# Two of the sample's turns beside the first projections instead of three, and the second chunk's first weights fetched with its rows

## The chip, the cores and the metric

One core of a Trainium2 chip runs the kernel. It has a matrix engine (TensorE, PE in the profile, with PEld for its weight loads), VectorE (DVE), ScalarE (ACT), GpSimd (POOL) and a queue that issues most transfers (SyncE, SP). The metric is the device time of one launch in microseconds (us), the median of several runs.

## What is computed

One inference step of a four-part hybrid decoder, for a prompt of 2048 tokens and a sample of 8 sequences with 8 new tokens each, whose 4096 past keys and values lie in a paged cache. Width 1024, 16 heads of 64. A recurrent layer comes first, then keys, values and forget gates are projected once, then one attention layer reads them. Cut to what matters here:

```python
def run_group(x, ...):
    y = recurrent_mixer(rms_norm(x, a_pre_norm), ..., a_w_in, ..., a_w_out)   # causal conv, RG-LRU, gate
    x = x + rms_norm(y, a_post_norm)
    k, v, logf = shared_kv(x, kv_norm, w_kv, b_f)
    # the sample's keys: cache_k[page_table] with the new rows behind them; the same for v and logf
    z = rms_norm(x, b_pre_norm) @ b_w_in
    q, g = z[..., :D_ATTN], z[..., D_ATTN:]
    s = q @ k.T * HEAD_DIM ** -0.5 + cq - ck          # cumulated log forget gates, causal mask
    o = softmax(s) @ v
    return x + rms_norm((o * silu(g)) @ b_w_out, b_post_norm), k, v, logf, ...
```

## The kernel before

Products with weights are made of three matmuls each, on high and low halves of both operands (lines 383 to 385), so each weight is fetched (`fetch`, line 415, tile `wst`) and then split in two (`wh` on ACT, `wl` on DVE or POOL). `Feed` (line 444) holds a list of weights in the order of their use: its `fetch` starts loads as far as the staging pool named in `wpool` has free buffers, and its `take` splits what is not yet split.

The prompt goes through the recurrent layer in two chunks of 1024 tokens (the first with the sample's 64 rows). The program's stages, in order:

- the recurrent layer of the first chunk (`recur`, `phase_a1`, then `phase_a2`);
- the first projections (`shared`, `phase_b`): keys, queries, values and gates of the first chunk. The generator yields after each group of 24 matmuls, 120 steps in all. The groups are called `kv` (rows as output) and `qg` (features as output); gates leave through tile `tgb` to `sgd` (line 974);
- the recurrent layer of the second chunk, the projections of two further chunks of 512, attention over 64 units, and the last projection.

The sample's attention against its cache is cut into 16 turns (a sequence and half of the heads each, `decode`, line 1043). A turn loads 32 pages of keys and 32 of values of 256 KB each (tile `raw`, line 1093), turns the keys on DVE (`ktr`, line 1180), makes scores (`dS`, line 1148), a softmax and products (`dO`, line 1262), and ends with a small product `dres` (line 1290). `FIRST` of the turns stand beside the first projections, from step 41 on: `Side.along` (line 1029) takes steps of the turns in proportion to the cost of the projections' steps, at a share that grows with `FIRST`, so that the turns' cost is used up about ten steps before `LEFT` = 16 steps remain. The other turns stand beside the later projections and attention, again in proportion to cost (`SHARE`, `SPAN`), and end before attention does.

When the first turns are recorded, their pool is closed (line 1817), and on its memory come the second chunk's staging pool for weights (`stage2`, line 1818) and its rows (`Norm0`, line 1819, tile `xt`, loaded at line 544, scaled at line 568, transposed on PE at line 524 into `tps`). `AHEAD` = 8 steps of the projections are then recorded, the first rows are transposed, and the rest of the projections follows. `recur` makes the feed for the recurrent layer's input weights and fetches from it as its first action, after all that.

The order within each engine's queue is not the order of the code: the framework records the instructions and a scheduler sorts them by a timeline that it simulates. On the chip each engine and each queue takes its instructions strictly in that order.

Of the kernel before, what the change touches and what calls it, by code (L numbers as in the profile page):

```python
# [22 lines left out]
KB = 8  # L23
# [28 lines left out]
SHARE0 = 2.0  # L52
LEFT = 16
AHEAD = 8
FIRST = 3
NACC = 5
NP = 6
ADD = "G"
# [29 lines left out]
def tile_hawk_fox(  # L88
# [72 lines left out]
    def super_chunks(sizes, width):  # L161
        assert sum(sizes) == SEQ
        return [SC(i, sum(sizes[:i]), n, width) for i, n in enumerate(sizes)]

    sca, scb = super_chunks(CHUNKS_A, 384), super_chunks(CHUNKS_B, 512)
# [56 lines left out]
    def sbuf(es, name, side=None):  # L222
        return es.enter_context(tc.tile_pool(name=name, bufs=1, side=side, reuse_waits="tile"))
# [165 lines left out]
    wpool = {"st": sbuf(stage, "stage", "right"), "ns": 3}  # L389
# [12 lines left out]
    class Weights:  # L402
# [28 lines left out]
        def ready(self):  # L431
            while len(self.t) < 2:
                if len(self.st) == len(self.t):
                    self.fetch()
                self.split()
            return self
# [66 lines left out]
    def alloc_x(pool, cols, g=""):  # L503
        return tuple(pool.tile([P, KB, cols], F32R, name=f"x{x}", tag=f"x{x}{g}") for x in "hl")

    def alloc_groups(pool, s, lo, hi):
        return [alloc_x(pool, s.groups[g][1], g) for g in range(lo, hi)]
# [1233 lines left out]
    a_in = [[(0, a_w_in[0, :, n * P:(n + 1) * P]), (P, a_w_in[0, :, D + n * P:D + (n + 1) * P])] for n in range(KB)]  # L1741
# [4 lines left out]
        todo[0][0].append((256, w_kv[:, 2 * D:]))  # L1746
        return todo

    def recur(s, a0, xs, covered, ex, out, then, begin, ready=None):

        with ExitStack() as ek:
            wk = sbuf(ek, f"a1_{s.i}")
            xs.extend(alloc_groups(sbuf(ex, f"xa_{s.i}"), s, len(xs), len(s.groups)))
            feed = Feed([(a_in[n],) for n in range(KB)])
            feed.fetch()
            feed.fetch()
            if ready:
                ready()

            def turnover():  # L1760
                ex.close()
                then()

            phase_a1(s, xs, a0, covered, feed, wk, out, turnover, begin)
# [11 lines left out]
    def steps(gen, n):  # L1776
        for _ in range(n):
            next(gen)
# [3 lines left out]
    a00 = Norm0(sca[0], sbuf(es0, "a0_0", "right"))  # L1782
    todo = a00.norm(2)
    out = Out(a_w_out[0], 4)
    x0, a2 = [], []
# [4 lines left out]
        out.place(sbuf(wo, "wo_0", "right"))  # L1790

    xs = []
    recur(sca[0], a00.turned(xs, todo), xs, 0, ExitStack(), out, turn0, lambda: next(a2[0]), prologue)
    x0.extend(alloc_x(sbuf(xe0, "xb0"), scb[0].cols))
    drain(a2[0])
    wo.close()
    turns = [(b, 0) for b in range(FIRST)]
    turns += [(b, hg) for b in range(DB) for hg in range(2) if (b, hg) not in turns]
# [14 lines left out]
    dec = ExitStack()  # L1813
    side = Side(decode(dec, turns[:FIRST], 2, 2, False))
    side.along(gen, FIRST * TURN / 320000 * SHARE0, 120 - done - LEFT)
    side.upto(1e12)
    dec.close()
    wst = sbuf(stage, "stage2", "right")
    a01 = Norm0(sca[1], sbuf(es1, "a0_1", "right"))
    todo = a01.norm(3)  # L1820
    ex, xs = ExitStack(), []
    xs.extend(alloc_groups(sbuf(ex, "xg_1", "right"), sca[1], 0, 1))
    steps(gen, AHEAD)
    a01 = a01.turned(xs, todo)
    covered = next(a01)
# [6 lines left out]
    out = Out(a_w_out[0], 4)  # L1832
    x1, a2 = [], []
    lim, end = scb[1].g0, scb[1].g0 + scb[1].cols

    def turn1():
# [2 lines left out]
                           lambda g: (*(t[:, (g - lim) // P] for t in x1), 0) if g < end else (g - end,)))  # L1839
        out.place(sbuf(wo, "wo_1", "right"))  # L1840

    recur(sca[1], a01, xs, covered, ex, out, turn1, lambda: next(a2[0]))
    xpool = sbuf(xe1, "xb1")
    x1.extend(xpool.tile([P, scb[1].cols // P, KB, P], F32R, name=f"x{x}", tag=f"x{x}") for x in "hl")
    drain(a2[0])
# [16 lines left out]
    def beside():  # L1862
        yield from decode(dec, turns[FIRST:], 4, 2, True)
        dec.close()
        dec_done.append(True)
        yield from project_ready(last)

    side = Side(beside())
    share = SHARE * (16 - FIRST) * TURN / (1024 / 128 * 24 * 4112 * 0.42 + 950000)
    side.along(gen, share)  # L1870
# [4 lines left out]
    cost = sum(4.1 * 0.42 * (512 - max(0, k - qc * 4) * P) + 213 for qc in range(4) for k in range(4 * qc + 4)) * H  # L1875
    side.along(attention(att), ((16 - FIRST) * TURN - side.spent) / (cost * SPAN))
    place.clear()
# [14 lines left out]
def build(inputs):  # L1892
    import numpy as _np
    import concourse.bacc as _bacc
    import concourse.tile as _tile
    from concourse import mybir as _mybir

    nc = _bacc.Bacc("TRN2", target_bir_lowering=False, num_devices=1)
    arrays, args = {}, []
    for name in _INS:  # L1900
        a = _np.ascontiguousarray(inputs[name])
        arrays[f"in_{name}_dram"] = a
        args.append(nc.dram_tensor(f"in_{name}_dram", a.shape, _mybir.dt.from_np(a.dtype), kind="ExternalInput").ap())
    for i, shape in enumerate(_OUTS):
        args.append(nc.dram_tensor(f"out_{i}_dram", shape, F32, kind="ExternalOutput").ap())
    with _tile.TileContext(nc, schedule_with_timeline_sim=True) as tc:
        tile_hawk_fox(tc, *args)
    return nc, arrays
# [8 lines left out]
```

## Time and profile before

| | us |
|---|---|
| median of 3 runs | 3024.01 |
| lowest and highest run | 3018.45, 3026.65 |
| span of the profiled execution (first to last instruction) | 3014.0 |
| the profiled execution's own time (launch to end) | not recorded beside its span |
| mean granted clock of TensorE | 0.970 of full speed |

A table by group of instructions gives their busy time, the mean of one, and the idle time of the engine just ahead of them with what ended it. The timeline gives start, duration, engine, line, operation, and the tiles (written <- read), with the count of equal neighbours. A table of stretches gives for each stretch the busy time of every engine, the granted clock, the share of time in which the 16 transfer engines were busy, and what they moved. A profile lists each matmul on 32-bit data of dS, dO and their like as two entries, so the program's order has half as many.

### The profile page before, as it was taken

The numbers are of one execution on the slowest core, as the hardware profiler recorded it, in microseconds if no ns is written. First come the engines' busy times: TensorE is split into PE (matmuls) and PEld (weight loads), VectorE is DVE, ScalarE is ACT, GpSimd is POOL, SyncE is SP. The second block draws the span as 40 slices with busy tenths as digits, with TensorE's granted clock in tenths as the row PEclk, the third lists the DMA queues.
The fourth block names the chain that finished last, engine by engine and source line by source line (L and its number), as shares of the span: only waits on it lengthen the run. The fifth ranks groups of instructions, "written<-read, shape, count | busy, mean of one in ns | idle before, by whom it ended". The sixth has DMA issues, their size and how long they took to land.

```text
span 3014.0 us, 60435 instructions
## 1 busy us (share of the span) xinstructions
PE 2787.3 (92%) x21614; PEld 2240.2 (74%) x21614; DVE 1802.1 (60%) x4013; ACT 1268.1 (42%) x2874; POOL 1084.5 (36%) x1198
## 2 busy tenths in 40 slices
PE   5998999999987999999999689999899999999998
PEld 5997789989877997888889456666566556566687
DVE  7877465424427775676564466767566656655344
ACT  4665342222125665534333234444444444355311
POOL 1653201000003653100000246666575756569522
PEclk9999999999998999999999889999999999999999
DMA  4224546889863226699999868888699877874343
GB/s 123 83 85 134 175 124 195 251 275 282 269 218 92 90 90 194 210 318 344 340 334 322 271 225 243 258 282 285 212 290 292 268 251 252 275 249 122 95 148 111
DMA packets 472958, 653.78 MB, mean 217 GB/s; under 512 B 91291, under 2 KB 268828, under 8 KB 465381
## 3 DMA queue, kind: packets, MB, share of 16 engines
q1 hardware_dynamic: 470950, 644.26, 67.2%
q10 hardware_dynamic: 1420, 3.56, 0.4%
q8 instruction: 171, 2.80, 0.4%
q0 software_dynamic: 288, 2.10, 0.2%
q14 instruction: 129, 1.06, 0.1%
HBM read 514.22 MB, written 135.16 MB: 215 GB/s over the span
## 4 chain that ended last, share of the span: by engine, by line
PE 59%; DMA 17%; DVE 9%; ACT 5%; SPq 4%; issue 3%; POOL 2%; DVEq 0%; ACTq 0%; POOLq 0%
PE ops L1622 6%; DMA raw<-in_cache_k_dram 5%; PE y L383 4%; PE st L1594 4%; PE y L384 4%; PE y L385 4%; PE sx L1429 4%; PE dO L1262 3%; PE kv L383 3%; PE kv L384 3%; PE kv L385 3%; PE st L1595 3%; PE dS L1148 3%; DMA raw<-in_cache_v_dram 3%; PE qg L383 2%
## 5 line engine op out<-in xcount | busy, mean ns | idle before, releaser
L108 POOL TENSOR_TENSOR acc<-acc,p 128x512 f32<-128x512 f32 (+3 forms) x543 | 599.3, 1105 | 331.4 <-PE ops L1622 143.4
L1609 ACT ACTIVATE p<-st 128x512 f32<-128x512 f32 (+2 forms) x553 | 278.0, 526 | 394.4 <-PE st L1595 187.4
L1180 DVE STREAM_TRANSPOSE ktr<-raw 128x1024 f32<-128x1024 f32 x256 | 307.8, 1225 | 126.1 <-DMA raw<-in_cache_k_dram 115.6
L1431 DVE TENSOR_REDUCE mxs<-sx 128x1 f32<-128x512 f32 x384 | 254.0, 681 | 144.4 <-PE sx L1429 143.5
L384 PE MATMUL kv<-wl,xh 128*128 128x256 f32 (+3 forms) x1088 | 307.6, 285 | 5.6 <-DVE wl L428 5.6
L383 PE MATMUL kv<-wh,xh 128*128 128x256 f32 (+3 forms) x1088 | 308.1, 287 | 4.5 <-ACT wh L427 4.5
L385 PE MATMUL kv<-wh,xl 128*128 128x256 f32 (+3 forms) x1088 | 307.4, 284 | 2.5 <-DMA xl<-xld 2.5
L1594 PE MATMUL st<-qa,ka 128*128 128x512 f32 (+3 forms) x640 | 269.7, 423 | 11.3 <-ACT p L1609 8.7
L1429 PE MATMUL sx<-kbt,qbt 96*128 96x512 f32 (+3 forms) x640 | 225.6, 413 | 48.5 <-DMA qbt<-qd 30.8
L1622 PE MATMUL ops<-p,vvt 128*64 128x256 f32 (+1 forms) x2090 | 253.3, 369 | 0.7 <-ACT p L1609 0.4
L1113 POOL TENSOR_TENSOR qw<-qb,amask 128x128 f32<-128x128 f32 x64 | 31.2, 493 | 606.5 <-PE dS L1148 313.0
L427 ACT ACTIVATE wh<-wst,gv 128x256 fp32r<-128x256 f32 (+1 forms) x384 | 164.5, 499 | 197.3 <-DMA wst<-in_b_w_in_dram 59.7
L428 DVE SCALAR_TENSOR_TENSOR wl<-wst,gv,wh 128x256 fp32r<-128x256 f32 (+1 forms) x384 | 169.0, 494 | 129.5 <-ACT wh L427 113.3
L1595 PE MATMUL st<-qbt,kbt 128*128 128x512 f32 (+3 forms) x640 | 236.6, 371 | 0.1
L383 PE MATMUL qg<-xh,wh 128*128 128x512 f32 (+2 forms) x640 | 229.0, 359 | 0.0
L385 PE MATMUL qg<-xh,wl 128*128 128x384 f32 (+2 forms) x640 | 227.9, 357 | 1.1 <-DVE wl L428 1.1
L384 PE MATMUL qg<-xl,wh 128*128 128x512 f32 (+2 forms) x640 | 227.7, 357 | 0.0
L1622 PEld LDWEIGHTS ops<-p,vvt 128*64 128x64 f32 x2090 | 155.2, 141 | 84.2 <-issue 20.0
L383 PEld LDWEIGHTS kv<-wh,xh 128*128 128x128 f32 (+1 forms) x1088 | 201.5, 187 | 11.6 <-ACT wh L427 6.2
L384 PEld LDWEIGHTS kv<-wl,xh 128*128 128x128 f32 (+1 forms) x1088 | 202.0, 187 | 9.7 <-DVE wl L428 6.5
L385 PEld LDWEIGHTS kv<-wh,xl 128*128 128x128 f32 (+1 forms) x1088 | 203.2, 187 | 4.3 <-DMA xl<-xld 2.9
L1594 PEld LDWEIGHTS st<-qa,ka 128*128 128x128 f32 x640 | 124.2, 194 | 104.1 <-issue 51.1
(307 smaller groups left out, 6399.2 us busy)
## 6 DMA issues: line engine op xcount, KB each, us to landing
raw<-in_cache_k_dram SPq DMA_DIRECT2D x512, 256.0 KB
raw<-in_cache_v_dram SPq DMA_DIRECT2D x512, 256.0 KB
wst<-in_w_kv_dram SPq DMA_DIRECT2D x48, 512.0 KB
wst<-in_b_w_in_dram SPq DMA_DIRECT2D x48, 512.0 KB
xt<-in_x_prompt_dram SPq DMA_DIRECT2D x32, 512.0 KB
wst<-in_a_w_in_dram SPq DMA_DIRECT2D x64, 256.0 KB
out_dram<-kf SPq DMA_DIRECT2D x128, 128.0 KB
sc<-cd SPq DMA_DIRECT2D x16, 1024.0 KB
```

The source lines that it names most:

```text
L108: eng.tensor_tensor(out, a, b, op=op)
L383: T.matmul(ps, lh(k), rh(k), start=(k == 0), stop=False)
L384: T.matmul(ps, lh(k), rl(k), start=False, stop=False)
L385: T.matmul(ps, ll(k), rh(k), start=False, stop=(k == nk - 1))
L428: V.scalar_tensor_tensor(wl[:, k, :], st[:, k, :], gk, f(wh[:, k, :]), op0=ALU.mult, op1=ALU.subtract)
L1180: behind("V", V.transpose(t.kts[pp][:, n], raw[:, :, pp * 256:(pp + 1) * 256]).ins)
L1429: T.matmul(ps[:, :w], qb[0:96, j * P:(j + 1) * P], kb[0:96, ck * 512:ck * 512 + w], start=True, stop=True)
L1431: place["V"] = V.reduce_max(mx[:, j, ck:ck + 1], ps[:, :w], axis=AX.X).ins
L1594: place["T"] = T.matmul(ps[:, lo:], ka[:, ks], qa[:, lo:], start=True, stop=False).ins
L1595: T.matmul(ps[:, lo:], kb[:, ks], qb[:, lo:], start=False, stop=(k < qc * 4))
L1609: pair.append((k, lo, p, A.activation(p[:, lo:], ps[:, lo:], AF.Exp)))
L1622: return T.matmul(ops[r * HD:(r + 1) * HD, a0 * P:], vvs[h % 2][:, k, :], p[:, :].rearrange("p (a r c) -> p a r c", a=2, r=2)[:, a0:, r, : ...
```

## The change

`FIRST` becomes 2: the third turn leaves the first projections and joins the others, which become 14. The shares of both sides are formulas in `FIRST` and change with it. The feed of the second chunk's recurrent layer is made and asked to fetch directly behind the allocation of its rows, into `stage2`, and handed to `recur`; the staging pool of the projections still to be recorded is put back after that.

```diff
-FIRST = 3
+FIRST = 2
...
-    def recur(s, a0, xs, covered, ex, out, then, begin, ready=None):
+    def input_weights():
+        feed = Feed([(a_in[n],) for n in range(KB)])
+        feed.fetch()
+        feed.fetch()
+        return feed
+
+    def recur(s, a0, xs, covered, feed, ex, out, then, begin, ready=None):
...
-            feed = Feed([(a_in[n],) for n in range(KB)])
-            feed.fetch()
-            feed.fetch()
+            feed = feed or input_weights()
...
-    recur(sca[0], a00.turned(xs, todo), xs, 0, ExitStack(), out, turn0, lambda: next(a2[0]), prologue)
+    recur(sca[0], a00.turned(xs, todo), xs, 0, None, ExitStack(), out, turn0, lambda: next(a2[0]), prologue)
...
     xs.extend(alloc_groups(sbuf(ex, "xg_1", "right"), sca[1], 0, 1))
+    of_b, wpool["st"], wpool["ns"] = dict(wpool), wst, 3
+    feed = input_weights()
+    wpool.update(of_b)
     steps(gen, AHEAD)
...
-    recur(sca[1], a01, xs, covered, ex, out, turn1, lambda: next(a2[0]))
+    recur(sca[1], a01, xs, covered, feed, ex, out, turn1, lambda: next(a2[0]))
```

Three places in the order of the built programs. First, SP's queue around the second chunk's rows (`xt`), before: behind the last pages of the third turn come the last three stores of gates, then rows and weights.

```order
L1093 DMA raw<-in_cache_v_dram 128x512
L974 DMA sgd<-tgb 128x256
L974 DMA sgd<-tgb 128x384
L683 DMA gst<-in_a_w_ga_dram 128x128
L684 DMA gst<-in_a_w_gx_dram 128x128
L974 DMA sgd<-tgb 128x384
L544 DMA xt<-in_x_prompt_dram 128x1024
L536 DMA apreB<-in_a_pre_norm_dram 128x1024
L544 DMA xt<-in_x_prompt_dram 128x1024 x3
L415 DMA wst<-in_a_w_in_dram 128x4x128 x6
```

The same queue in the changed program, from the second store behind the last pages of the second turn on:

```order
L974 DMA sgd<-tgb 128x384
L415 DMA wst<-in_b_w_in_dram 128x4x256
L544 DMA xt<-in_x_prompt_dram 128x1024
L536 DMA apreB<-in_a_pre_norm_dram 128x1024
L544 DMA xt<-in_x_prompt_dram 128x1024
L974 DMA sgd<-tgb 128x256
L544 DMA xt<-in_x_prompt_dram 128x1024 x2
L415 DMA wst<-in_a_w_in_dram 128x4x128 x6
L974 DMA sgd<-tgb 128x384 x2
L974 DMA sgd<-tgb 128x256
L974 DMA sgd<-tgb 128x384
L415 DMA wst<-in_b_w_in_dram 128x4x256
```

Rows and input weights now stand ahead of 17 of the stage's stores and of the last weight of the gates.

Second, PE's queue at the end of the first projections, before (`u` and `g` are the recurrent layer's first products):

```order
L383 MATMUL qg<-xh,wh 128x384
L384 MATMUL qg<-xl,wh 128x384
L385 MATMUL qg<-xh,wl 128x384
L1290 MATMUL dres<-sel,ob 128x16 x4
L524 MATMUL tps<-ident,xt 128x128 x24
L383 MATMUL u<-xh,wh 128x384
L383 MATMUL g<-xh,wh 128x384
```

In the changed program the last turn's `dres` has 219 `qg` matmuls between it and the first eight transposes; the last eight of the first 24 stand like this among the projections:

```order
L384 MATMUL qg<-xl,wh 128x384
L385 MATMUL qg<-xh,wl 128x384
L383 MATMUL qg<-xh,wh 128x320
L384 MATMUL qg<-xl,wh 128x320
L524 MATMUL tps<-ident,xt 128x128 x4
L385 MATMUL qg<-xh,wl 128x320
L524 MATMUL tps<-ident,xt 128x128 x4
L383 MATMUL qg<-xh,wh 128x320
```

From there to the last `qg` are 141 more, and `u` follows it directly; in all 411 `qg` stand between `dres` and `u`, where there were none.

Third, PE's queue at the start of attention (`sx`, the first pass over the scores), before and then changed:

```order
L384 MATMUL qg<-xl,wh 128x512
L385 MATMUL qg<-xh,wl 128x512
L1226 MATMUL dsum<-ddg,ones 128x64
L1429 MATMUL sx<-kbt_19861,qbt_19862 128x128
L1429 MATMUL sx<-kbt_19861,qbt_19862 128x256
```

The changed queue has the scores of a turn where the sum of a softmax stood:

```order
L385 MATMUL qg<-xh,wl 128x512
L1148 MATMUL dS<-ktr,qw 32x128 x32
L1163 MATMUL dS<-sy,qw 32x8 x16
L1148 MATMUL dS<-ktr,qw 32x128 x32
L1429 MATMUL sx<-kbt_19536,qbt_19537 128x128
```

Counted over these rows, 656 instead of 576 dS and 198 instead of 188 dO stand between the recurrent layer and attention's first `sx`, and 1360 instead of 1296 and 726 instead of 670 behind it.

## The prediction

> **What bounds the kernel now.** I read the page's first part, then a table of stretches cut at the stages, then the timeline at the seam between the first chunk's projections and the second chunk's recurrent layer, because both edits act there. First the page:
>
> ```profile
> PE 2787.3 (92%) x21614; PEld 2240.2 (74%) x21614; DVE 1802.1 (60%) x4013; ACT 1268.1 (42%) x2874; POOL 1084.5 (36%) x1198
> ```
>
> TensorE (PE) is the busiest engine by far, so time is won or lost where PE works less or stands still. The table of stretches has, after the length, the busy time of PE, PEld, DVE, ACT and POOL with instruction counts, then granted clock, DMA share and GB/s:
>
> ```profile
> 520.00:893.00 373.00, 351.52 (x3491) 330.26 (x3489) 147.99 (x265) 89.89 (x244) 7.09 (x23) 1.00 0.83 258
> 893.00:926.00 33.00, 9.14 (x40) 7.69 (x40) 18.15 (x45) 15.64 (x34) 10.94 (x7) 0.59 0.83 250
> ...
> 1290.00:1707.00 417.00, 407.28 (x3744) 351.91 (x3742) 258.43 (x507) 156.45 (x404) 21.71 (x35) 1.00 0.99 327
> 1707.00:1748.00 41.00, 8.86 (x23) 4.93 (x27) 8.81 (x29) 2.44 (x9) 8.28 (x13) 0.54 0.91 241
> 1748.00:2720.00 972.00, 918.23 (x8323) 585.39 (x8317) 634.07 (x1342) 442.96 (x1094) 599.48 (x569) 0.97 0.82 260
> 2720.00:2840.00 120.00, 117.19 (x661) 77.94 (x658) 56.29 (x115) 61.44 (x133) 92.37 (x81) 0.96 0.31 94
> ```
>
> From 520 to 893 the first chunk's projections run with three of the sample's turns beside them; from 1290 to 1707 the later projections, and from 1748 attention, run with the other thirteen. PE is busy 94 to 98% in all three, so a turn costs its PE time wherever it stands. Two holes remain: 893 to 926 and 1707 to 1748. The first is the seam. PE's timeline there (start, us, operation, count, and in brackets the idle time before it and what ended it):
>
> ```profile
> 892.67 0.96 PE L1290 MATMUL dres<-sel,ob 128*128 128x16 f32 x8
> 910.03 1.97 PE L524 MATMUL tps<-ident,xt 128*128 128x128 f32 x8 [16.40 <-DVE xt L568]
> 917.05 1.97 PE L524 MATMUL tps<-ident,xt 128*128 128x128 f32 x8 [5.05 <-DVE xl L108]
> 921.42 2.21 PE L524 MATMUL tps<-ident,xt 128*128 128x128 f32 x8 [2.41 <-DVE xl L108]
> ...
> 932.71 1.03 PE L524 MATMUL tps<-ident,xt 128*128 128x128 f32 x8
> 934.85 1.32 PE L524 MATMUL tps<-ident,xt 128*128 128x128 f32 x8 [1.10 <-DVE xl L108]
> 939.17 1.97 PE L524 MATMUL tps<-ident,xt 128*128 128x128 f32 x8 [3.00 <-DVE xl L108]
> ```
>
> PE ends the third turn (dres) at 893.6 and then waits for the second chunk's rows, normalised on DVE. Why so late is in the timeline of the other queues:
>
> ```profile
> 879.58 2.02 SPq L1093 DMA_DIRECT2D raw<-in_cache_v_dram  x4
> 882.60 5.87 SPq L974 DMA_DIRECT2D sgd<-tgb  x2
> ...
> 894.40 0.42 SPq L544 DMA_DIRECT2D xt<-in_x_prompt_dram  x1
> ...
> 897.08 7.69 SPq L415 DMA_DIRECT2D wst<-in_a_w_in_dram  x6
> ```
> ```profile
> 908.69 5.91 DVE L568 SCALAR_TENSOR_TENSOR xt<-xt,nr_y,apreB 128x1024 f32<-128x1024 f32 x3
> ```
> ```profile
> 908.79 3.40 POOL L108 TENSOR_TENSOR wl<-wst,wh 128x1024 fp32r<-128x1024 f32 x1 [12.08 <-ACT wh L101]
> ```
>
> The third turn's last pages are asked for at 880, its last product is at the very end of the projections, and rows and input weights, which take over the turns' buffers, are asked for only after that: 894.4 and 897.1. Loading, squaring and scaling three rows' tiles takes to 914.6, twenty microseconds with nothing left for PE.
>
> **The change, part by part.** *(a) One turn leaves the first stage.* PE's work for a turn is the key scores (dS) and the value products (dO). The table of stretches for each alone (length, PE, PEld, DVE or ACT busy, clock, DMA), dS first, then dO:
>
> ```profile
> 520.00:893.00 373.00, 25.56 (x864) 23.85 (x864) 8.79 (x15) 1.00 0.83 258
> 1290.00:1712.00 422.00, 35.98 (x1152) 31.35 (x1152) 11.74 (x20) 0.99 0.99 327
> 1748.00:2720.00 972.00, 83.73 (x2592) 73.17 (x2592) 26.71 (x45) 0.97 0.82 260
> ```
> ```profile
> 520.00:893.00 373.00, 26.33 (x396) 12.05 (x396) 1.09 (x3) 1.00 0.83 258
> 1290.00:1712.00 422.00, 25.57 (x376) 10.54 (x376) 0.73 (x2) 0.99 0.99 327
> 1748.00:2720.00 972.00, 94.42 (x1340) 37.78 (x1332) 4.08 (x11) 0.97 0.82 260
> ```
>
> A turn is 288 dS and 132 dO entries. In the first stage it costs (25.56 + 26.33)/3 = 17.3 us. The waits of PE ahead of these groups, and ahead of the projections' own matmuls, in 520 to 893:
>
> ```profile
> L383 PE MATMUL kv<-wh,xh 128*128 128x256 f32 (+1 forms) x504 | 142.3, 285 | 2.3 <-ACT wh L427 2.3
> L384 PE MATMUL kv<-wl,xh 128*128 128x256 f32 (+1 forms) x504 | 142.3, 284 | 2.9 <-DVE wl L428 2.9
> ...
> L1262 PE MATMUL dO<-raw,sx 128*32 128x256 f32 x384 | 25.1, 384 | 7.7 <-DMA raw<-in_cache_v_dram 4.2 <-issue 1.3 <-DMA vd<-kf 1.2
> L1148 PE MATMUL dS<-ktr,qw 128*32 128x128 f32 x768 | 22.4, 273 | 3.8 <-DVE ktr L1180 3.8
> ```
>
> So (7.7 + 3.8)/3 = 3.8 of waiting goes too: **-21.1**. The projections' own waits, 2.3 + 2.9 = 5.2, come of sharing ACT, DVE and the DMA with the turns; between 0 and -5.2, and I take a third, **-1.7**.
>
> *(b) It comes back later.* The order rows put 80 more dS and 10 more dO ahead of attention, 64 and 56 inside it; each is two trace entries. Before attention: 160 x 35.98/1152 + 20 x 25.57/376 = 6.4. Inside: 128 x 83.73/2592 + 112 x 94.42/1340 = 12.0. The waits in attention:
>
> ```profile
> L1262 PE MATMUL dO<-raw,sx 128*32 128x256 f32 x1296 | 88.6, 394 | 13.2 <-DMA raw<-in_cache_v_dram 13.2
> L1148 PE MATMUL dS<-ktr,qw 128*32 128x128 f32 x2304 | 73.1, 281 | 3.3 <-DVE oTs L108 3.3
> ```
>
> At that rate 112/1296 x 13.2 + 128/2304 x 3.3 = 1.3 more. Together **+19.7**. The turn's small products (dm, dsum, dres) and its exponentials go and come alike. Its 64 page loads of 256 KB stay on the same queue, only later; whether the DMA has room is not in this sum. Lower bound 0, since these stages hardly wait for pages; upper bound, if pages bind, in the rivals. I take **+2**, near the waits seen.
>
> *(c) The seam.* With two turns the second ends, in the order, 411 projection matmuls before the stage's end. Their pace:
>
> ```profile
> 860.00:893.00 33.00, 26.43 (x148) 24.27 (x148) 3.19 (x6) 2.93 (x7) 1.00 0.69 224
> ```
>
> 26.43/148 = 0.18 us each, so some 74 us of PE work lie behind the turn and 219 x 0.18 = 39 us between it and the first transpose of rows. Loading and scaling took 20 us at the seam; it fits beneath. The window 893 to 926 holds 9.14 of PE work at clock 0.59, worth 5.4 at full clock, so 27.6 of its 33.0 go. Of the next rows' waits (1.10 and 3.00) I take half, 2, since two transpose buffers still pace them. Against this stands a wait of 0 to 4.5: the first weights have their data early, but their second half needs a buffer that the stage's last weights hold until their last use, and then POOL's 3.40 (the row above) and ACT's rounding of about 1; the first half's 24 matmuls cover most. I take 2. Together **-27.6**, from -32 to -23.
>
> The Trainium skill, "TensorE: Matmul & The Clock Gate", "HAM oscillation", says only an idle stretch of more than about 3.4 us halves the clock, so by the page a residual wait of 2 costs 2 and no more. The rows at 932.71 and 939.17 show eight transposes at 1.03 without a wait and 1.97 after 3.00, so by the trace it could cost 0.9 on top, and the sum would be -26.7.
>
> The six weight loads of the second edit pass about eighteen stores of gates and the last weights on SP's queue. If SP stands at a load because a turn's buffer is not free, stores behind it wait, then the gate buffers, then PE: the cover is the four PSUM buffers of a group each, 24 x 0.18 = 4.3 us a group, some 17 us; past that each microsecond is PE's. By the order the turn is over by then, so I cost it at 0.
>
> *(d) The other hole*, 1707 to 1748, waits for attention's first keys behind page traffic. Another phase of a turn will stand there (scores instead of exponentials and their scattered stores). I have no row for that phase: -10 to +10, value 0.
>
> **Sum** against the profiled execution: -21.1 - 1.7 + 19.7 + 2 - 27.6 = -28.7, span 3014.0 to 2985.3. The median of the runs, 3024.0, lies 10.0 above the span (start and end around it, which no row shows); I keep that: **2995 us**.
>
> **Rivals.** *The seam stays.* The second turn lags on the chip as the third did (its V pages landing late), or rows and weights still come after the last store. Then only -1.1 remains: 3023. For it: now, too, the end of the turns is a matter of pages. Against: 411 matmuls of distance instead of none. A half closed seam gives 3009.
>
> *Attention becomes bound by the turns' pace: slower.* PE takes its queue in order, so if a turn cannot run faster than now, attention stretches to hold more of them. Two turn ends there:
>
> ```profile
> 2567.72 1.02 PE L1290 MATMUL dres<-sel,ob 128*128 128x16 f32 x8
> ...
> 2664.38 0.96 PE L1290 MATMUL dres<-sel,ob 128*128 128x16 f32 x8
> ```
>
> 96.7 us a turn. Inside attention 0.44 of a turn's scores and 0.85 of its products are added, 0.65 on the mean: 63 us instead of 13.3, so +21 in all: 3045. It decides from about 29 us of added waiting. Against it: PE waits 16.5 us for dS and dO in 972, so the turns have slack now; for it, the DMA share is 0.82 there and 0.99 in the stage ahead. The DMA view of 1290 to 1707 in 40 slices:
>
> ```profile
> GB/s 301 370 294 284 360 327 326 267 303 332 403 358 389 379 376 279 333 368 398 259 358 320 261 359 338 369 352 331 328 305 284 373 322 318 309 363 355 355 208 174
> ```
>
> Slices of 403 and 398 against a mean of 327 show room. The Trainium skill, "DMA: Bandwidth & Descriptors", "Specifications", gives about 358 GB/s from HBM for one core; taken as a limit it would leave this stage 31 GB/s and make the rival likelier; the slices above it, stores included, say it isn't one here.
>
> **How the numbers follow.** Forecast 0.72, 2995, own range 2978 to 3007 by its bounds; half closed seam 0.09, 3009; seam stays 0.12, 3023; attention slower 0.07, 3045. About 0.3% is what a measurement of this kernel tells from no change, 9 us: faster means below 3015, which the first two give, 0.81; same 0.12; slower 0.07. The range runs from 2978 to 3022, leaving out the last case, part of the third and the forecast's low tail.
>
> **What would show it.** Right: no idle above 3 us on PE where tps first stands, transposes between qg matmuls, clock near 1.00 through the seam, wst<-in_a_w_in issued some 60 us before the last gate store; dS x576 and dO x264 in the first projections; waits before dO in attention near 15. Wrong: a tps wait of over 10 us, dS or dO waits in attention that double, or a hole before attention that grows beyond 50.

## The result, and the profile after

| | before | changed |
|---|---|---|
| median of 6 runs each, us | 3021.23 | 2999.76 |
| lowest to highest | 3014.74 to 3031.76 | 2996.61 to 3001.49 |
| span of the profiled execution | 3014.0 | 2998.0 |

The ratio is 0.994, with a 95% interval of 0.9919 to 0.996: 0.4 to 0.8% faster, 18 us by the ratio and 21 by the medians. The forecast was 2995.

The page's first part for the changed kernel: PE does the same work as before.

```profile
PE 2789.2 (93%) x21614; PEld 2245.0 (75%) x21614; DVE 1800.9 (60%) x4013; ACT 1265.0 (42%) x2874; POOL 1078.6 (36%) x1198
```

The table of stretches, with the columns as before (length, PE, PEld, DVE, ACT, POOL, clock, DMA share, GB/s):

```profile
800.00:875.00 75.00, 75.00 (x467) 74.63 (x464) 37.55 (x95) 30.79 (x72) 4.33 (x8) 1.00 0.49 157
875.00:910.00 35.00, 31.03 (x177) 29.42 (x176) 19.28 (x39) 13.18 (x26) 8.82 (x13) 0.90 0.21 62
1208.00:1673.00 465.00, 449.45 (x3988) 387.62 (x3987) 289.88 (x608) 175.85 (x448) 22.73 (x49) 0.99 0.98 324
1673.00:1710.00 37.00, 9.65 (x173) 6.98 (x171) 12.50 (x32) 1.08 (x2) 8.80 (x14) 0.64 0.92 289
1710.00:2690.00 980.00, 915.31 (x8475) 584.46 (x8474) 642.14 (x1362) 436.83 (x1094) 587.37 (x564) 0.97 0.85 270
```

The seam lies at 875 now. PE is busy without a break in the 75 us ahead of it, and 31 of the 35 us behind it; where 33 us held 9 us of work at clock 0.59 before, the clock is now 0.90. The queue of transfers shows why:

```profile
804.11 0.46 SPq L544 DMA_DIRECT2D xt<-in_x_prompt_dram  x1
...
807.55 8.02 SPq L415 DMA_DIRECT2D wst<-in_a_w_in_dram  x6
...
878.56 0.46 SPq L974 DMA_DIRECT2D sgd<-tgb  x1
```

Rows and first weights are asked for at 804 and 808, 71 us and more ahead of the last gate store, not behind it. What PE still waits for between 860 and 905 (operation, releaser, total us, times, longest):

```profile
PE tps L524 <- DVE xl L108: 3.8, 3, 1.8
PE u L383 <- ACT xh L101: 0.2, 1, 0.2
```

The stages of the two profiled executions, cut at the first or last matmul of a kind (us; holes are the time from the last `qg` to the next matmul of the following stage, `u` or `sx`, the first of them counted within the column before it; the last column runs from the last score to the end):

| | start | first kv to u of chunk 2 | its hole | second recurrent layer | later projections | hole before sx | attention | end |
|---|---|---|---|---|---|---|---|---|
| before | 395.4 | 527.9 | 30.5 | 331.0 | 451.3 | 31.0 | 1080.2 | 197.2 |
| changed | 398.9 | 476.5 | none | 333.3 | 464.6 | 26.0 | 1101.6 | 197.1 |
| difference | +3.5 | -51.4 | | +2.3 | +13.3 | -5.0 | +21.4 | -0.1 |

The first stage with the seam gives 51.4. The late stages take 32.0 of it back (+2.3 +13.3 -5.0 +21.4). The table of stretches for dS alone and then for dO alone says how much of this is the turn's own work:

```profile
520.00:875.00 355.00, 17.96 (x576) 16.29 (x576) 5.89 (x10) 0.99 0.77 236
1208.00:1710.00 502.00, 42.80 (x1312) 37.52 (x1312) 13.41 (x23) 0.96 0.98 322
1710.00:2690.00 980.00, 85.64 (x2720) 75.17 (x2720) 28.04 (x47) 0.97 0.85 270
```
```profile
520.00:875.00 355.00, 17.55 (x264) 8.02 (x264) 0.75 (x2) 0.99 0.77 236
1208.00:1710.00 502.00, 27.12 (x398) 10.91 (x398) 1.09 (x3) 0.96 0.98 322
1710.00:2690.00 980.00, 103.87 (x1452) 42.17 (x1452) 4.06 (x11) 0.97 0.85 270
```

Against the rows of before, dS and dO take 8.7 and 11.0 us more from the later projections on (128.44 against 119.71, and 130.99 against 119.99), 19.7 in all. From the first `kv` of the later projections to the last score, 1562.6 us before and 1592.2 now, PE is busy 16.7 us more (1464.2 and 1480.9) and idle 12.9 more, with some 5 us of the added work inside the old hole. Groups of PE in 1204 to 1690 (first row) and in 1699 to 2801 (the others), with busy time, mean ns, and the idle time ahead of them:

```profile
L1148 PE MATMUL dS<-ktr,qw 128*32 128x128 f32 x1152 | 36.9, 282 | 7.9 <-DVE ktr L1180 7.5 <-DVE cn L108 0.3
...
L1594 PE MATMUL st<-qa,ka 128*128 128x512 f32 (+3 forms) x640 | 269.1, 422 | 22.3 <-ACT p L1609 13.3 <-DMA qa<-qd 8.5
L1622 PE MATMUL ops<-p,vvt 128*64 128x256 f32 (+1 forms) x2080 | 249.7, 367 | 4.1 <-ACT p L1609 3.3 <-ACT yo L1609 0.3
...
L1429 PE MATMUL sx<-kbt,qbt 96*128 96x512 f32 (+3 forms) x640 | 228.3, 413 | 27.9 <-DMA qbt<-qd 19.8 <-DVE mxs L1431 2.5 <-ACT qbt L1448 2.1
L1262 PE MATMUL dO<-raw,sx 128*32 128x256 f32 x1408 | 97.8, 399 | 20.2 <-DMA raw<-in_cache_v_dram 20.1
```

and two of the attention groups in the kernel before, 1736 to 2817:

```profile
L1594 PE MATMUL st<-qa,ka 128*128 128x512 f32 (+3 forms) x640 | 269.7, 423 | 11.3 <-ACT p L1609 8.7 <-DMA qa<-qd 1.4 <-ACT x L1609 0.3
L1429 PE MATMUL sx<-kbt,qbt 96*128 96x512 f32 (+3 forms) x640 | 225.6, 413 | 48.5 <-DMA qbt<-qd 30.8 <-DVE mxs L1431 7.9 <-DVE mxs L1433 7.2
```

One line of the waits of PE in the later projections (1209 to 1673) belongs to the first of these rows:

```profile
PE dS L1148 <- DVE ktr L1180: 7.5, 2, 6.3
```

The reader is to see three kinds: a single stand of 6.3 us for turned keys in the later projections, the turn's own waits in attention (dO 13.2 before, 20.2 now), and attention's own scores (`st`), whose work is the same and whose waits doubled, from 11.3 to 22.3. Against the last kind stands the first pass over the scores (`sx`): without its wait for `qd`, which is nearly all the hole before attention, it waited 17.7 before and 8.1 now.

### The profile page after: what moved, and what is told of

Same layout as the page of the kernel before. It is cut to its first block, busy times and chain, and to the rows that moved or that the text cites. A ratio compares the mean times of both kernels' runs of the same rounds, so it can differ in the third digit from the quotient of the medians.

```text
span 2998.0 us, 60402 instructions
## 1 busy us (share of the span) xinstructions
PE 2789.2 (93%) x21614; PEld 2245.0 (75%) x21614; DVE 1800.9 (60%) x4013; ACT 1265.0 (42%) x2874; POOL 1078.6 (36%) x1198
## 3 DMA queue, kind: packets, MB, share of 16 engines
q1 hardware_dynamic: 470758, 644.13, 67.5%
## 4 chain that ended last, share of the span: by engine, by line
PE 50%; DMA 17%; DVE 5%; ACT 4%; SPq 4%; issue 3%; POOL 2%; ACTq 0%; DVEq 0%; POOLq 0%
PE ops L1622 6%; DMA raw<-in_cache_k_dram 5%; DMA raw<-in_cache_v_dram 4%; PE st L1594 3%; PE sx L1429 3%; PE dO L1262 3%; PE y L383 3%; PE y L384 3%; PE y L385 3%; PE kv L384 3%; PE kv L385 3%; PE kv L383 3%; PE dS L1148 3%; PE st L1595 2%; PE qg L383 2%
## 5 line engine op out<-in xcount | busy, mean ns | idle before, releaser
L1594 PE MATMUL st<-qa,ka 128*128 128x512 f32 (+3 forms) x640 | 269.1, 422 | 22.3 <-ACT p L1609 13.3
L383 PE MATMUL qg<-xh,wh 128*128 128x384 f32 (+2 forms) x640 | 229.3, 359 | 0.0
L1622 PEld LDWEIGHTS ops<-p,vvt 128*64 128x64 f32 x2090 | 154.5, 140 | 85.1 <-issue 17.7
```

The source lines that it names most:

```text
L383: T.matmul(ps, lh(k), rh(k), start=(k == 0), stop=False)
L1594: place["T"] = T.matmul(ps[:, lo:], ka[:, ks], qa[:, lo:], start=True, stop=False).ins
L1622: return T.matmul(ops[r * HD:(r + 1) * HD, a0 * P:], vvs[h % 2][:, k, :], p[:, :].rearrange("p (a r c) -> p a r c", a=2, r=2)[:, a0:, r, : ...
```

## The experiments

Four kernels were timed on one chip with the kernel before, which had a median of 3014.4 us there; `no_feed` turned out to be the changed program itself and serves as its time (3001.8). Two further sets of four had the kernel before at 3014.0 and 3015.3, so the medians can be read side by side. The stages of all, in the same cuts, and the ratio to the kernel before with its interval:

| run | median | ratio (95%) | span | first kv to u | hole | later projections | hole | attention | end |
|---|---|---|---|---|---|---|---|---|---|
| no_feed | 3001.8 | 0.995 (0.9933 to 0.9968) | 2998.3 | 473.0 | none | 465.0 | 27.4 | 1108.5 | 197.1 |
| lag | 3024.2 | 1.0029 (1.0013 to 1.0046) | 3026.0 | 498.9 | 30.9 | 466.2 | 27.6 | 1107.8 | 197.1 |
| drop | 2968.1 | 0.9852 (0.983 to 0.9875) | 2957.8 | 472.8 | none | 454.6 | 29.4 | 1074.8 | 197.1 |
| one_first | 3035.9 | 1.0069 (1.0045 to 1.0093) | 3037.7 | 451.5 | none | 483.1 | 28.2 | 1141.6 | 201.4 |
| half_pages | 3017.3 | 1.0019 (1.0001 to 1.0037) | 3008.7 | 474.0 | none | 487.5 | 18.3 | 1097.5 | 201.7 |
| half_drop | 2968.0 | 0.9843 (0.9818 to 0.9867) | 2962.4 | 472.0 | none | 478.1 | 20.8 | 1061.1 | 201.7 |
| in_att | 2989.3 | 0.9921 (0.9897 to 0.9944) | 2987.2 | 472.2 | none | 455.5 | 28.5 | 1100.7 | 201.7 |
| longer | 2983.5 | 0.989 (0.9869 to 0.9912) | 2995.2 | 475.6 | none | 465.1 | 28.9 | 1093.4 | 201.7 |
| before_longer | 3005.7 | 0.9969 (0.9947 to 0.999) | 3013.4 | 527.3 | 30.7 | 454.2 | 31.2 | 1071.3 | 201.4 |
| drop_longer | 2957.7 | 0.9788 (0.9761 to 0.9814) | 2959.5 | 476.4 | none | 453.1 | 29.6 | 1067.6 | 201.7 |
| both | 3005.3 | 0.996 (0.9945 to 0.9975) | 3004.9 | 473.1 | none | 455.3 | 30.0 | 1115.3 | 201.4 |
| both_more | 2997.0 | 0.9939 (0.9918 to 0.996) | 2991.8 | 472.0 | none | 454.6 | 29.0 | 1081.9 | 222.5 |

### Is the gain the seam? (lag)

```diff
-SHARE0 = 2.0
-LEFT = 16
+SHARE0 = 1.3
+LEFT = 9
```

> Two turns beside the first projections as in the change, but slowed (SHARE0 1.3, LEFT 9), so that the second turn's last product is again the last thing before the second chunk's row transposes, with no projection matmul between them. Seam theory (the gain is the work between the last turn and the rows; moving a turn is itself a small loss): the hole at the seam is back, about 25 to 31 us from the last qg to the first u, and the time is 27 to 31 us above the change, near 3028, not faster than before. Relief theory (the first stage was overfull, and the gain is having one turn less in it): the time stays within 5 us of the change, near 3000.

Measured: 22.4 us above `no_feed` by the medians, 27.7 by the spans, and 0.3% slower than the kernel before. PE's timeline at its seam, and the stretch:

```profile
863.77 0.96 PE L1290 MATMUL dres<-sel,ob 128*128 128x16 f32 x8
883.43 1.97 PE L524 MATMUL tps<-ident,xt 128*128 128x128 f32 x8 [18.69 <-DVE xt L568]
890.43 1.97 PE L524 MATMUL tps<-ident,xt 128*128 128x128 f32 x8 [5.04 <-DVE xl L108]
892.95 2.21 PE L524 MATMUL tps<-ident,xt 128*128 128x128 f32 x8 [0.55 <-DVE xl L108]
```
```profile
864.00:897.00 33.00, 8.72 (x38) 7.28 (x38) 19.86 (x42) 15.13 (x31) 9.86 (x7) 0.56 0.82 243
```

The hole is the one of before (16.40 and 5.05 of waiting there, 18.69 and 5.04 here, clock 0.56), although one turn less stands in the stage. So the hole belongs to the distance between the last turn and the rows, not to the number of turns, and without closing it, moving the turn loses. The relief theory falls. By the medians the time came out a little below the 27 to 31 of the seam theory.

### Does the early fetch matter? (no_feed)

```diff
-    recur(sca[1], a01, xs, covered, feed, ex, out, turn1, lambda: next(a2[0]))
+    recur(sca[1], a01, xs, covered, ex, out, turn1, lambda: next(a2[0]))
```

with the other lines of the second edit taken out as well.

> FIRST = 2 alone, without the early fetch of the input weights. By the order of the instructions on all five engines this is the changed program itself, since the scheduler puts the weights' loads behind the rows' in both: within 0.15% of the change, near 3000. If the second edit did matter, as the prediction took it to (weights ahead of about eighteen stores): the first u waits for its weights, 5 to 10 us more than the change, near 3008.

Measured: 0.995 against 0.994 of the change, one inside the other's interval, and spans of 2998.3 and 2998.0. In the order, no instruction and no wait differs between the two on any of the five engines; the same holds for the kernel before with and without the early fetch. The likely reason is that the scheduler puts the loads where their buffers come free, and that the end of the turns decides that. The second edit does nothing.

So the two traces, of `no_feed` and of the change, are of one program, and they show how far one execution's stages scatter: against the kernel before, the first stage is 54.9 us shorter here and 51.4 there, and the stages from the second recurrent layer to the end of attention are 39.0 longer here and 32.0 there.

### What does a late turn cost? (drop, one_first)

```diff
+    G.memset(oTs[:, :, :], 0.0)
...
+    turns.remove((2, 0))
...
-    share = SHARE * (16 - FIRST) * TURN / (1024 / 128 * 24 * 4112 * 0.42 + 950000)
+    share = SHARE * (15 - FIRST) * TURN / (1024 / 128 * 24 * 4112 * 0.42 + 950000)
```

and likewise 15 for 16 in the share of attention.

> The change with one of the fourteen later turns left out altogether (the first half of the heads of the third sample sequence is not computed; its rows of the output are zeros), so that as many turns stand behind the first projections as in the kernel before. Against the change it gives what one late turn costs. The prediction's sum (6.4 + 12.0 + 1.3 of waits + 2): 20 to 22 us below the change, near 2979. The traces' own difference (13 us in the later projections and 21 in attention, less 5 at the hole): about 30 us below the change, near 2970. If late turns lie in slack (PE waits for other things in attention anyway): under 12 us below, near 2990.

Measured: 33.7 us below `no_feed` by the medians, 29.5 by the ratios (0.0098 of 3014), 40.5 by the spans. That is the traces' 30 or more, not the prediction's 20 to 22 and not slack. By stages, 10.4 of it lies in the later projections and 33.7 in attention, less 2.0 at the hole. The scores' waits are back at 11.6 (1685 to 2761):

```profile
L1595 PE MATMUL st<-qa,ka 128*128 128x512 f32 (+3 forms) x640 | 268.0, 420 | 11.6 <-ACT p L1610 8.7 <-DMA qa<-qd 1.5 <-ACT x L1610 0.5
```

```diff
-FIRST = 2
+FIRST = 1
```

> FIRST = 1: one turn beside the first projections, fifteen later. The seam has 288 projection matmuls ahead of the rows, so it is closed as in the change. Seam theory: nothing is left to win there, and only the price of moving a second turn shows: by the prediction's sum (21.1 + 1.7 gone, 19.7 + 2 come) -1, near 2999; by the traces of before and after (about 30 to 34 come) +8 to +12, near 3010. Relief theory: another 15 to 20 us faster than the change, near 2982.

Measured: 34.1 us above `no_feed` by the medians, so both theories missed, the relief theory by its sign. The first stage again gave what it was priced at, 473.0 less 451.5 = 21.5, with no seam left to close. So this second moved turn cost some 56 us late (34.1 + 21.5), against 30 to 34 for the first. PE in 1695 to 2690 shows where the pages come in:

```profile
L1262 PE MATMUL dO<-raw,sx 128*32 128x256 f32 x1344 | 93.7, 397 | 32.6 <-DMA raw<-in_cache_v_dram 29.3 <-DMA sx<-pd 1.7 <-issue 1.0
```

The second moved turn costs more than the first, and dO's waits rise with it: 13.2, 20.2, 32.6.

### Is it the page traffic? (half_pages, half_drop)

```diff
-                page = cache[ds(regs[i], 1), :, hg * 8:(hg + 1) * 8, :]
-                d = S.dma_start(raw[:, i, :], page.rearrange("o k h d -> (o k) (h d)"))
+                n = 4 if ahead else 8
+                page = cache[ds(regs[i], 1), :, hg * 8:hg * 8 + n, :]
+                d = S.dma_start(raw[:, i, :n * 64], page.rearrange("o k h d -> (o k) (h d)"))
```

where `ahead` is true for the late turns alone, and with the readers of `raw` taking the first 256 columns for both halves; the second kernel has this edit on top of `drop`.

> The change, with the late turns' page loads half as wide (4 of 8 heads; the scores and products of the other half read the same columns, so every instruction of PE, DVE and ACT stays as long, and those heads' results are not computed). Pages theory (the waits behind the added turn, dO's on raw and attention's own on qa, come of a DMA that has no room for more pages beside the prefill's transfers): PE's waits for raw in attention (20 us in the change) fall below 5, those in the later projections (dS 7.5) below 2, and the time is 15 to 30 us below the change, near 2978. Density theory (a turn's steps put their DVE and ACT work between attention's, so its chains of sx, p and mps come late however fast the pages are): within 8 us of the change, near 2996.

> Half as wide page loads and one late turn left out (both as above), to read the price of a late turn where pages are cheap: half_pages less this run. Pages theory: 17 to 22 us, the work and small waits of the prediction's sum. Density theory: 30 to 38 us, as with whole pages (33.7 by the medians, 40.5 by the spans).

Measured: 15.5 us above `no_feed`, where the pages theory gave 15 to 30 below the change and the density theory within 8 of it. A late turn still costs 49.3 by the medians (3017.3 less 2968.0) and 46.3 by the spans, where they gave 17 to 22 and 30 to 38. So both theories miss, and the pages theory falls as the price of the turn. Of its first step one half came as expected, dO's waits for pages below 5; the other did not, since the waits for turned keys in the later projections came to 6.1 instead of below 2. The edit halves the bytes of a page and leaves the number of loads and packets (470758 on the main queue, here and in the change), so a cost that goes by their number isn't tested. dO's waits in 1710 to 2690, and the stretch of the later projections:

```profile
L1263 PE MATMUL dO<-raw,sx 128*32 128x256 f32 x1408 | 96.7, 397 | 4.6 <-DMA raw<-in_cache_v_dram 4.6
```
```profile
1204.00:1691.00 487.00, 459.23 (x4048) 395.93 (x4046) 290.23 (x611) 176.09 (x447) 22.07 (x50) 0.96 0.81 249
```

and that stretch in the changed kernel:

```profile
1209.00:1673.00 464.00, 448.45 (x3984) 386.78 (x3982) 288.88 (x606) 174.88 (x446) 22.73 (x49) 0.99 0.98 325
```

With the rate lower by a quarter and a DMA share of 0.81 instead of 0.98 the stage is 23 us longer, in `half_drop` too (478.1 against 454.6). PE is idle 27.8 us in it instead of 15.6, and the largest of these waits are for VectorE's halves of weights (`wl`, 11.3 us, in the change 1.2), not for DMA. The scheduler sets another order for the shorter loads, so a comparison with the change itself holds two edits; the pair with and without the turn holds one, and that pair says that the pages' width isn't what makes the turn dear. Removing 15.6 us of dO's waits for pages shortened attention by only 4 to 11.

### Where does the added turn go best? (in_att, longer, and what they add up to)

```diff
-SHARE = 1.13
+SHARE = 1.05
```

> The change with SHARE 1.05 instead of 1.13: as many scores and products stand before attention's first sx as in the kernel before (576 and 188), and the whole added turn runs inside attention. If the stage with a DMA share of 0.98 is the dear place (13 us for a fifth of a turn): 5 to 10 us faster than the change, near 2993. If attention is the dear place (its own waits grow by 16 us for two thirds of a turn): 5 to 10 us slower, near 3008.

Measured: 12.5 us below `no_feed` by the medians (intervals of the ratios overlap slightly). The later projections fell to 455.5, near before's 451.3, and attention, though it took the whole turn, did not grow (1100.7 against 1101.6 and 1108.5). So in this pair a fifth of a turn in the later projections cost more than it did inside attention.

```diff
-SPAN = 0.9
+SPAN = 0.97
```

> The change with SPAN 0.97 instead of 0.9, so that the turns beside attention are spread over more of it. Density theory: fewer steps per unit of attention, so shorter chains and 5 to 10 us less, near 2992, as long as the turns still end before attention does. Pages theory: the same or somewhat less, 2990 to 3000, since the page traffic is spread too. If the turns now end behind attention, what is left of them is bare: 3010 or more.

Measured: 18.3 us below `no_feed`, where the density theory gave 5 to 10, and 1.1% faster than the kernel before: the fastest of the kernels that compute everything. Its trace is of its slowest execution (2997.2; the others 2974.7 to 2985.5), so its attention of 1093.4 is rather a high reading. dO's waits in 1710 to 2690 went with page loads unchanged in width:

```profile
L1262 PE MATMUL dO<-raw,sx 128*32 128x256 f32 x1280 | 87.5, 395 | 5.0 <-DMA raw<-in_cache_v_dram 4.6 <-DMA raw<-in_cache_k_dram 0.4
```

The same edit was then made to the kernel before and to `drop`:

> The kernel before (three turns first, open seam) with SPAN 0.97 instead of 0.9. Room theory (what a late turn costs beyond its work comes of packing it into the first nine tenths of attention; with thirteen turns there is less to pack): 3 to 9 us faster than the kernel before, against 18 for the same edit on the change. General theory (a longer spread helps any version alike): 15 to 20 us faster than the kernel before.

> SPAN 0.97 in the kernel with one late turn left out, to read the price of a late turn at the longer spread, as longer (2983) less this one. Room theory: the price falls to 17 to 24, the prediction's sum, so this is 2959 to 2966, 2 to 9 below drop. General theory: the price stays 31 to 37, so this is 2946 to 2952, 16 to 22 below drop.

Measured: 9.6 us faster than the kernel before, just over the 3 to 9 of the room theory; 10.4 below `drop` by the medians, between the two theories, but 19 by the ratios (0.9852 to 0.9788), which is the general one. The price of a late turn at the longer spread is 25.8 by the medians and 30.7 by the ratios, against 33.7 and 29.5 at the shorter. Whether room in attention is what a late turn lacks is not settled by this.

Then SHARE 1.05 with SPAN 0.97, and with SPAN 1.03:

> The change with SHARE 1.05 and SPAN 0.97 together. If the two gains (12 and 18 us by the medians against no_feed) are of different places, the later projections and attention, they add up to 22 to 30 less than the change, near 2975. If the room in attention is one store from which both draw (SHARE 1.05 puts 0.2 of a turn more there), no better than longer alone, 2980 to 2988.

> SHARE 1.05 and SPAN 1.03, so that the turns end with attention itself: in the order 31 matmul rows are left behind the last turn instead of 231. Room theory: as good as both or up to 8 us better. Against: the last turn's late page or its dres waits stand bare at the end, and what follows attention waits for them: 5 to 15 us worse than both, near 2985.

Measured: 3005.3 and 2997.0. The two gains don't add up: `both` keeps the short projections (455.3), but its attention takes 1115.3, more than either alone, and neither expectation gave that. `both_more` has the shortest attention of all with fourteen late turns, 1081.9, and pays 21 us at the end (222.5 against 201.7), as expected of turns that end with attention, yet it is 8.3 us faster than `both`, the edge of what the room theory gave. Part of what it saves in attention has only moved behind the last score. Attention and the end together take 1302 us in `in_att`, 1317 in `both` and 1304 in `both_more`, three kernels that differ only in how the turns are spread over attention, and their medians lie up to 16 us apart without going one way with the spread. That is a scatter as large as the 12 and 18 us of `in_att` and `longer`, so these two are measured facts about two orders, and no proof of a rule.

## Why the prediction was right, and which terms were off

**The first stage and the seam: right.** Forecast -21.1 -1.7 -27.6 = -50.4, measured -51.4 (-54.9 in the trace of `no_feed`). The parts were separated: taking one more turn out, where no seam was left, gave 21.5 (`one_first`), and opening the seam again cost 22.4 by time and 27.7 by span (`lag`). Loading and scaling the rows fits beneath the projections, as the 75.00 of 75.00 us show. The residual wait for the first weights, taken as 2 with bounds of 0 and 4.5, was 0.2. The signs named in advance came: transposes between `qg`, dS x576 and dO x264 in the first stage, weights asked for 71 us ahead of the last store, clock 1.00 up to the seam and 0.90 behind it; the waits of `tps` came to 3.8 in three pieces of at most 1.8. One sign did not come: dO's waits in attention, named near 15, were 20.2. And the sum counted no loss of clock beside so short waits, but the trace has one: around `tps` waits of 1.8, 0.8 and 1.2 us the granted clock was 0.50 from 887.8 to 894.7.

**The second edit: credited with what the first does.** The prediction let "the six weight loads of the second edit" pass eighteen stores. They do pass them, but because the turn ends earlier; `no_feed` is the same program without that edit. The sum doesn't suffer, since the seam was priced as a whole.

**The late turn: the term that was off.** The work was sized well, 18.4 in the sum (the small waits apart) and 19.7 in the trace. The step that failed is the waiting, "At that rate ... 1.3 more" and "I take +2": 3.3 in all, by the old waits of the turn's own groups. Behind it stands the premise that "a turn costs its PE time wherever it stands". Measured, PE was idle 12.9 us more between the first `kv` of the later projections and the last score (19.5 in the trace of `no_feed`). The late stages together grew by 32.0 where the sum had 21.7, and the three pairs with and without a late turn put its price at 26 to 49 by the medians, 30 to 53 by the ratios. By the stages of these pairs, 9 to 12 of it lie in the later projections, where the sum had 6.4, and 26 to 36 in attention, where it had 13.3. The prediction had bounds for the waiting, from 0 to the rival's 3045, and took a value next to the lower one.

What the prediction left out is what the turn does to the others: the dS of the later projections stood 7.5 for turned keys (`ktr`), nearly all in one wait, and attention's own scores waited 11 us more (`st`, 11.3 to 22.3). The second is no rule. The first pass waited 9.6 less at the same time, and only in the first pair do the waits of `st` fall by as much with the turn left out, from 21.3 in `no_feed` to 11.6. At the longer spread they fall from 20.5 to 17.5, and with narrow pages they rise from 16.0 to 23.1, while the price is there in all three. From the first late `kv` to the last score, the pairs differ by 7 to 20 us of idle PE and by 22 to 30 of busy PE, of which dS and dO explain about 20. So which group waits changes with the order, and no single mechanism of the price is shown.

**The hole before attention**, costed at 0 within 10 either way, shrank by 5.0, with 5 us of dS now inside it.

**The rivals.** The seam that stays did not happen, but `lag` shows what it would have been: 3024 measured, 3023 forecast. Attention bound by the turns' pace did not decide at 14 late turns; at 15 something of its kind is seen (`one_first`: dO's waits 32.6, 34 us slower than the change). That DMA bandwidth is the cause is not borne out. The Trainium skill, "DMA: Bandwidth & Descriptors", "Specifications", gives about 358 GB/s as the HBM limit of one core, half of a stack's 716. The later projections run at 325, and at 249, in `half_pages`, they took 23 us longer; the order differs there, so this rules no limit out, but it gives none any support. What exactly keeps attention's `st` waiting longer for `p`, the exponentials on ScalarE, beside a fourteenth turn stays open: it was not isolated.

**The step from span to time.** The prediction took 10.0 us of "start and end around it" on top of the span. Every run with both numbers shows 1.7 to 2.3 us. So most of the 10 was probably the profiled execution of before being quicker than its median, and the span's own error (2985.3 forecast, 2998.0 measured, 12.7 too low) was partly hidden by it: 2995 stands nearer to 2999.8 than its terms deserve, and that part of the hit is luck.

## What to carry to other kernels

A side job that ends with its stage also fixes when the next stage's loads can start, because those take over its buffers: look for the hole behind it, price the hole by what PE could do in it, and check in the built order how much work stands between the two. Moving the job has a price beyond its own instructions; read it by leaving one such job out altogether, since here its work was 20 us and its price 26 to 49, and the second one moved cost more than the first. And an edit that issues a load earlier in the code may change nothing where a scheduler sorts the queue by free buffers.

## What the runs showed of the hardware that was not expected

Executions of one program differ, and their times go with the granted clock. `longer` took 2974.7 us at a mean clock of 0.975 and 2997.2 at 0.971; the kernel before, on one chip, 3007.8 at 0.971 and 3027.3 at 0.965. Over the 21 runs of the kernel before there the correlation of time and clock is -0.69, and for the twelve experiments it lies between -0.35 and -0.88. Which of the two follows the other is not shown: where PE waits, the clock is low too, as at the seam. One profiled execution can so stand some 10 us from its kernel's median (13.7 in `longer`, 8.3 in `drop`), as much as the wait that is being looked for, and differences between spans of two kernels carry that error on top.
